# A list scheduler learns that VectorE and GpSimd share a port, and layer 1 takes its heads in another order

## The chip, the cores and the metric

The kernel runs on one core of one Trainium2 chip. The metric is the device time of one execution in microseconds (us), as the median of three runs. The profile's names for the engines are used throughout: PE is TensorE (its matrix products), PEld its weight loads, DVE is VectorE, ACT is ScalarE, POOL is GpSimd, SP is the queue that issues nearly all of the DMA transfers.

## The reference: what is computed

A trunk of two layers on a sequence of 512 rows of 1024 numbers, in float32. Both layers have the form

```python
h = rmsnorm(x, norm_mix[layer])
x = x + mixer(h)                       # even_mixer in layer 0, odd_mixer in layer 1
x = x + squared_relu_mlp(rmsnorm(x, norm_mlp[layer]), w_up[layer], w_down[layer])
```

and a last `rmsnorm` ends it. The part that matters here is the mixer of layer 1:

```python
qc, kc, vc, c_q, c_kv, k_r = split(h @ w_in)                 # 512, 512, 512, 384, 256, 32 columns
o_c = stick_breaking_attention(qc, kc, vc)                   # 8 heads of 64
q_full = rmsnorm(c_q, q_norm) @ w_uq                         # 8 heads of 64 + 32
kv_full = rmsnorm(c_kv, kv_norm) @ w_ukv                     # 8 heads of 64 + 64
o_d = mla_attention(q_nope, rope(q_rope), k_nope, rope(k_r), v_d)
o = concatenate([o_c, o_d]) @ w_out
# stick-breaking weights of a row: a = sigmoid(z) * (product of sigmoid(-z) over all later keys before the row)
```

`c_q` and `c_kv` are the latent compressions. The mixer of layer 0 has eight heads with a forgetting bias and eight with a relative-position bias, each with a softmax over its row.

## The kernel before, in words

**Numbers in two parts.** Products run on float32r operands, and each operand is kept as a rounded high part and the low part that is left, so a product of two matrices is three products on PE (`mm3`, L426). To make the two parts, ACT copies the high one and DVE subtracts it. For every 128x1024 block of weights that arrives by DMA as `wr`, this is one ACT copy to `wh` and one DVE subtraction to `wl` (`load_w`, L432). The blocks lie in a ring of eight buffers, so the split of a block waits until the products of an earlier one are done.

**The steps of layer 1.** The string `LAYER_1` (L29) is a list of names, and `step` (L1192) records the operations of each name:
- `v`: the values of the eight stick-breaking heads;
- `q0` to `q3` (`qk_pair`, L637): queries and keys of a pair of heads, 2 times 24 products of 512 columns;
- `s0` to `s7` (`stick_head`, L1171): one stick-breaking head. For each of four row blocks of 128 rows: two score products (`sc`) on PE, two sigmoids on ACT (`k` and `p`), two masks on POOL (AFFINE_SELECT), a running product along the row on DVE (a scan over `k`), and the product of `p` and `k` on POOL. Then ten transposes (`tr`) on PE, their split into two parts (`pt`) on ACT and DVE, eight products with the values (`av`), and the addition of the halves (`o`) on DVE;
- `cq` and `ck` (`c_proj`, L1110): the two compressions, 96 products of 384 columns and 96 of 288;
- `nq` and `nk` (`c_norm`, L1119): their norms, four row blocks each: a power of -1/2 of one number a row on POOL (`sm<-sm,mhalf`), a scaling on DVE (`ex<-u,sm,gain`), transposes on PE, a split (`u<-tr,u`);
- `kr`, `qr`, `qn`, `kn`, `vd`: rotated key, queries, keys and values of the latent heads from the normed compressions, with the weights of `wq` and `wkv`;
- `m0` to `m7`: the latent heads; `oc`, `od` and a last part ("end" below): the output projection; `x`: the residual is read back.

**What sets the order.** Nothing is issued as it is recorded. `Plan.schedule` (L133) is a list scheduler: it takes the recorded operations with their dependences, gives each engine the ready operation that was recorded first (those of the heads and norms count as 4000 places earlier, `urgent`), adds a cost from a table (`Op.cost`, L303), and frees buffers when their last use ends. The result is one fixed order for each engine, which then runs in that order: an operation that waits holds up all that stand behind it on its engine. The scheduler's times play no part on the chip; only its order does.

Of the kernel before, what the change touches and what calls it, by code (L numbers as in the profile page):

```python
# [25 lines left out]
WARM = 60  # L26
WARM2 = 12
LAYER_0 = """v a0 f0 f1 a1 a2 f2 f3 a3 f4 f5 f6 b0 f7 b1 c0 c1 b2 c2 b3 c3 x of c4 c5 c6 oc c7"""
LAYER_1 = """v cq q0 s0 nq ck s1 q1 kr s2 s3 nk q2 q3 wq qr0 qr1 qn0 qn1 qn2 qn3 wkv kn0 kn1 kn2 kn3 s4 s5 s6 vd0  # L29
 s7 vd1 vd2 vd3 x m0 m1 m2 m3 m4 m5 oc m6 od m7"""  # L30
Q_LORA, KV_LORA = 384, 256
NEG = -1.0e30
BIG = 3.0e38
# [25 lines left out]
class Plan:  # L59
# [73 lines left out]
    def schedule(self):  # L133
        self.depend()
        ops = self.ops
        for t in self.tag_of.values():
            if t.first is not None:
                t.slot.queue.append(t)
        for s in self.slots.values():
            s.queue.sort(key=lambda t: t.first)  # L140
        free_at = dict.fromkeys(self.ENGINES, 0.0)
        soon = {e: [] for e in self.ENGINES}
        ready = {e: [] for e in self.ENGINES}
        for i, op in enumerate(ops):
            if not op.left:
                heapq.heappush(soon[op.engine], (0.0, op.prio, i))
        order, dma_free, table = [], 0.0, None
        waiting = {}

        def wake(slot, now):  # L150
            for i in waiting.pop(slot, ()):
                heapq.heappush(soon[ops[i].engine], (now, ops[i].prio, i))

        while len(order) < len(ops):
            best = None
            for e in self.ENGINES:
                if ready[e]:
                    at = free_at[e]
                elif soon[e]:
                    at = max(free_at[e], soon[e][0][0])  # L160
                else:
                    continue
                if best is None or at < best[0]:
                    best = (at, e)
            assert best is not None, "the recorded order does not fit the tile pools"
            now, e = best
            while soon[e] and soon[e][0][0] <= now:
                _, p, i = heapq.heappop(soon[e])
                heapq.heappush(ready[e], (p, i))
            _, i = heapq.heappop(ready[e])  # L170
            op = ops[i]
            blocked = None
            fresh = [t for t in op.tiles if not t.placed]
            for t in fresh:
                s = t.slot
                if s.free_slots(now) <= 0 or (s.in_order and s.queue[s.head] is not t):
                    blocked = s
            if blocked is not None:
                late = blocked.next_free(now)
                if late is not None and (not blocked.in_order or any(  # L180
                        blocked.queue[blocked.head] is t for t in fresh)):
                    heapq.heappush(soon[e], (late, op.prio, i))
                else:
                    waiting.setdefault(blocked, []).append(i)
                continue
            for t in fresh:
                t.placed = True
                t.slot.take(now)
            cost = op.cost()
            if e == "scalar":  # L190
                want = TABLE.get(op.kw.get("func", op.args[2] if op.method == "activation" else None))
                if want is not None and want != table:
                    cost += 1300.0
                    table = want
            end = now + cost
            free_at[e] = end
            done = end
            if op.method == "dma_start":
                start = max(dma_free, end + 650.0)
                dma_free = start + op.dma_time()  # L200
                done = dma_free + 900.0
            order.append(i)
            for j in op.next:
                o = ops[j]
                lat = self.SEM if op.method == "dma_start" else self.LATENCY[e][o.engine]
                o.ready = max(o.ready, done + lat)
                o.left -= 1
                if not o.left:
                    heapq.heappush(soon[o.engine], (max(o.ready, now), o.prio, j))
            for t in fresh:  # L210
                wake(t.slot, now)
            for t in op.tiles:
                t.left -= 1
                t.end = max(t.end, done)
                if not t.left:
                    t.slot.give(t.end + self.SEM)
                    wake(t.slot, now)
        self.length = max(free_at.values())
        return order
# [68 lines left out]
class Op:  # L288
# [10 lines left out]

    def dma_time(self):  # L300
        return int(np.prod(self.outs[0].shape)) * 4 / 360.0

    def cost(self):  # L303
        if self.method == "dma_start":
            return 1000.0 if self.engine == "gpsimd" else 450.0
        n = self.width()
        if self.engine == "tensor":
            if self.method == "transpose":
                return 109.0
            m = int(np.prod(self.outs[0].shape[1:]))  # L310
            if self.outs[0].tensor.name.startswith("warm"):
                return 107.0
            return max(m / 2.4 + 13.5, 107.0)
        psum = any(a.space == bass.MemoryType.PSUM for a in self.ins)
        if self.engine == "scalar":
            c = n / 1.2 + (155.0 if n < 1024 else 140.0)
            if self.method == "activation" and isinstance(self.kw.get("bias"), bass.AP):
                c += 93.0
            return c + (188.0 if "accum_out" in self.kw else 0.0)
        if self.engine == "vector":  # L320
            if self.method in ("tensor_copy", "tensor_scalar", "memset") and not psum:
                return n / 1.92 + 100.0
            return n / 0.96 + (150.0 if n < 1024 else 100.0) + (83.0 if "accum_out" in self.kw else 0.0)
        if self.method == "tensor_tensor":
            return 599.0 if n == 1 else 2.1 * n + 150.0
        if self.method == "affine_select":
            return 430.0
        return 0.84 * n + (290.0 if self.method == "tensor_scalar" else 100.0)
# [45 lines left out]
def trunk(ctx, tc, x, positions, norm_mix, norm_mlp, norm_final, w_in_ab, b_forget, rel_bias,  # L374
# [888 lines left out]
    o = {}  # L1263
    for name in LAYER_1.split():
        step(name)
# [49 lines left out]
```

## Time and profile before

| | us |
|---|---|
| median of three runs | 1212.97 (1209.8 to 1214.74) |
| the profiled execution, its own time | 1213.36 |
| its span, first to last instruction | 1211.7 |
| PE busy | 1178.5 (97%) |
| DVE busy | 870.7 (72%) |
| ACT busy | 594.6 (49%) |
| POOL busy | 169.4 (14%) |

A busy PE is one that has a product under way; products are pipelined, so a PE that is busy can still be slower than it could be. In the trace nearly every operation has the line of the recording helper, so the names of what is written and read (`out<-in`) tell the operations apart. A stretch of the span can be asked for its busy times; layer 1's mixer lies between about 605 and 870 us.

### The profile page before, as it was taken

What the parts mean: (1) busy time and instruction counts of PE and PEld (TensorE: products, weight loads), DVE (VectorE), ACT (ScalarE), POOL (GpSimd) and SP (SyncE); (2) the same over time, 40 slices, a digit from 0 to 9 for tenths busy, and PEclk for the clock granted to TensorE, in tenths of its full rate; (3) what the DMA queues carried; (4) which work ended last, traced back from release to release, by engine and by line L of the source; (5) the groups of instructions that cost most, each with busy time, mean ns of one, the idle gap of its engine ahead of it and who ended that gap; (6) DMA issues with size and microseconds to landing.
All of it is one profiled execution on the core that took longest, in us unless ns stands there. A gap on an engine that the chain in (4) does not pass through costs nothing.

```text
span 1211.7 us, 16381 instructions
## 1 busy us (share of the span) xinstructions
PE 1178.5 (97%) x5958; PEld 993.0 (82%) x5958; DVE 870.7 (72%) x1466; ACT 594.6 (49%) x1064; POOL 169.4 (14%) x301
## 2 busy tenths in 40 slices
PE   9999999999999999999999998899899999999997
PEld 8987788888888888887899876688788888888886
DVE  6547788795876877777633899678768778787644
ACT  5346677534443444444424776556444434444423
POOL 2215522200000000000001576022100000000000
PEclk8999999999999999999999999899899999999999
DMA  5533334443143241225323212773521423321231
GB/s 196 158 96 96 88 93 162 137 151 121 35 139 105 74 153 43 62 70 160 111 76 100 79 53 72 171 197 77 207 86 39 156 85 98 128 69 36 72 102 70
DMA packets 101312, 127.89 MB, mean 106 GB/s; under 512 B 5272, under 2 KB 71200, under 8 KB 101232
## 3 DMA queue, kind: packets, MB, share of 16 engines
q1 hardware_dynamic: 101056, 126.55, 34.8%
q8 instruction: 47, 0.77, 0.3%
q0 software_dynamic: 176, 0.30, 0.1%
q14 instruction: 33, 0.27, 0.1%
HBM read 113.16 MB, written 4.23 MB: 97 GB/s over the span
## 4 chain that ended last, share of the span: by engine, by line
PE 64%; DVE 5%; DMA 3%; POOL 2%; issue 1%; ACT 1%; POOLq 0%; SPq 0%; DVEq 0%; ACTq 0%
PE mm L226 42%; PE pa L226 10%; PE pb L226 8%; POOL p L226 2%; PE tr L226 1%; DVE k L226 1%; PE sc L226 1%; PE av L226 1%; DVE wl L226 1%; DVE u L226 1%; DMA Qm<-u 1%; DVE pt L226 1%; DVE ex L226 1%; DMA Km<-u 1%; ACT wh L226 1%
## 5 line engine op out<-in xcount | busy, mean ns | idle before, releaser
L226 PE MATMUL mm<-u,wh 128*128 128x512 f32 (+1 forms) x1524 | 466.9, 384 | 4.1 <-DVE u L226 2.3
L226 PEld LDWEIGHTS mm<-u,wh 128*128 128x128 f32 x1524 | 279.7, 188 | 57.0 <-DVE u L226 4.4
L226 PE MATMUL mm<-u,wl 128*128 128x512 f32 (+1 forms) x762 | 292.2, 384 | 0.2 <-DVE wl L226 0.2
L226 PE MATMUL mm<-wh,u 128*128 128x512 f32 (+4 forms) x1008 | 269.6, 350 | 2.0 <-ACT u L226 2.0
L226 DVE TENSOR_TENSOR wl<-wr,wh 128x1024 fp32r<-128x1024 f32 (+5 forms) x152 | 175.3, 1157 | 88.2 <-ACT wh L226 86.5
L226 ACT CAST wh<-wr 128x1024 fp32r<-128x1024 f32 (+5 forms) x152 | 149.2, 987 | 156.2 <-PE mm L226 69.7
L226 PEld LDWEIGHTS mm<-wh,u 128*128 128x128 f32 x1008 | 178.3, 192 | 21.7 <-ACT u L226 2.3
L226 PE MATMUL mm<-wl,u 128*128 128x512 f32 (+4 forms) x504 | 177.0, 351 | 0.6 <-DVE wl L226 0.6
L226 PEld LDWEIGHTS mm<-u,wl 128*128 128x128 f32 x762 | 143.4, 188 | 26.2 <-DVE wl L226 0.9
L226 ACT CAST wh<-rw 128x1024 fp32r<-128x1024 f32 x84 | 88.5, 1054 | 114.3 <-PE mm L226 54.0
L226 DVE TENSOR_TENSOR wl<-rw,wh 128x1024 fp32r<-128x1024 f32 x84 | 102.8, 1223 | 57.0 <-ACT wh L226 56.5
L226 PEld LDWEIGHTS mm<-wl,u 128*128 128x128 f32 x504 | 96.9, 192 | 10.7 <-DVE wl L226 1.1
L226 POOL TENSOR_TENSOR sm<-sm,mhalf 128x1 f32<-128x1 f32 x28 | 21.4, 764 | 461.7 <-DVE sm L226 461.6
L226 POOL TENSOR_SCALAR p<-p,sm 128x128 f32<-128x128 f32 (+1 forms) x96 | 59.1, 616 | 177.1 <-DVE sm L226 143.8
L226 DVE TENSOR_TENSOR X<-mm,X 128x512 f32<-128x512 f32 x80 | 54.5, 686 | 30.4 <-PE mm L226 30.1
L226 PE MATMUL tr<-ident,p 128*128 128x128 f32 x320 | 65.3, 280 | 11.1 <-POOL p L226 10.7
L226 PE MATMUL pa<-wl,sh 128*128 128x512 f32 x192 | 74.7, 389 | 0.0
L226 PE MATMUL pa<-wh,sl 128*128 128x512 f32 x192 | 74.7, 389 | 0.0
L226 PE MATMUL pa<-wh,sh 128*128 128x512 f32 x192 | 74.4, 389 | 0.0
L226 ACT ACTIVATE sq<-ex 128x512 f32<-128x512 f32 x48 | 30.3, 630 | 86.3 <-DVE ex L226 86.3
L226 DVE SCALAR_TENSOR_TENSOR ex<-mm,rstd 128x512 f32<-128x512 f32 x64 | 44.0, 688 | 37.6 <-PE mm L226 33.7
L226 PE MATMUL av<-pt,u 128*128 128x512 f32 (+3 forms) x256 | 66.4, 342 | 0.6 <-ACT pt L226 0.5
(125 smaller groups left out, 1673.7 us busy)
## 6 DMA issues: line engine op xcount, KB each, us to landing
wr<-in_w_up_dram SPq DMA_DIRECT2D x64, 512.0 KB, 4.0
rw<-in_w_down_dram SPq DMA_DIRECT2D x48, 512.0 KB, 3.4
wr<-in_w_in_ab_dram SPq DMA_DIRECT2D x22, 512.0 KB, 4.2
wr<-in_w_down_dram SPq DMA_DIRECT2D x16, 512.0 KB, 3.3
wr<-in_w_in_cd_dram SPq DMA_DIRECT2D x11, 512.0 KB, 3.9
X<-in_x_dram SPq DMA_DIRECT2D x8, 512.0 KB, 6.2
wr<-in_w_out_ab_dram SPq DMA_DIRECT2D x8, 512.0 KB, 4.3
wr<-in_w_out_cd_dram SPq DMA_DIRECT2D x8, 512.0 KB, 4.2
```

The source lines that it names most:

```text
L226: getattr(getattr(self.nc, op.engine), op.method)(*op.args, **op.kw)
```

## The change

Two things, in one diff. The scheduler keeps a time `port_free`: an operation for which `Op.port` holds ends no earlier than `port_free - 200` ns plus its own cost, and then sets `port_free`. `port` holds for a GpSimd operation that reads a tile wider than one element a row from SBUF, and for a VectorE operation that reads two such tiles (one is enough for a copy or a scalar operation); tiles in PSUM don't count. And in `LAYER_1` the first two pairs of heads stand ahead of the compressions.

```diff
-LAYER_1 = """v cq q0 s0 nq ck s1 q1 kr s2 s3 nk q2 q3 wq qr0 qr1 qn0 qn1 qn2 qn3 wkv kn0 kn1 kn2 kn3 s4 s5 s6 vd0
- s7 vd1 vd2 vd3 x m0 m1 m2 m3 m4 m5 oc m6 od m7"""
+LAYER_1 = """v q0 s0 q1 s1 cq s2 nq ck s3 kr nk q2 s4 q3 wq qr0 qr1 qn0 qn1 qn2 qn3 wkv kn0 kn1 kn2 kn3 s5
+ vd0 vd1 vd2 vd3 s6 s7 x m0 m1 m2 m3 m4 m5 oc m6 od m7"""
...
-        order, dma_free, table = [], 0.0, None
+        order, dma_free, port_free, table = [], 0.0, 0.0, None
...
-            end = now + cost
+            if op.port():
+                end = max(now, port_free - 200.0) + cost
+                port_free = end
+            else:
+                end = now + cost
...
+    def port(self):
+
+        if self.engine not in ("vector", "gpsimd") or self.method == "dma_start":
+            return False
+        wide = [a for a in self.ins if a.space not in (bass.MemoryType.PSUM, bass.MemoryType.DRAM) and int(np.prod(a.shape[1:])) > 1]
+        return len(wide) > (self.engine == "vector" and self.method not in ("tensor_copy", "tensor_scalar"))
```

No operation is added or removed: both programs have the same 8871 recorded operations. On PE both start with the 192 products of `v`. Before, the row is `v`, the 96 of `cq`, the 48 of `q0`, then `ck`, among whose products the scores of `s0` and `s1` stand, then `q1`, `q2` with `s1` to `s3`, and `q3`, whose 14th product the scores of `s4` precede. Now it is `v`, `q0`, then `q1` and `cq` with `s0` to `s2` and the scores of `s3`, then `ck` with the rest of `s3`, then `q2`, and `q3`, of which 20 products stand ahead of the scores of `s4`. From `kn3` on both orders are nearly alike.

Three places. The first is POOL in layer 1. Before, the powers of `nq` (four rows of `sm<-sm,mhalf`) stand behind the last product of head `s1` (511 columns) and ahead of the masks of `s2`:

```order
L226 TENSOR_TENSOR p_1413<-p_1413,k_1414 128x383
L226 AFFINE_SELECT p_1416<-p_1416 128x128
L226 TENSOR_TENSOR p_1416<-p_1416,k_1417 128x511
L226 TENSOR_TENSOR sm_1370<-sm_1369,mhalf 128x1
L226 TENSOR_TENSOR sm_1376<-sm_1375,mhalf 128x1
L226 TENSOR_TENSOR sm_1382<-sm_1381,mhalf 128x1
L226 TENSOR_TENSOR sm_1388<-sm_1387,mhalf 128x1
L226 AFFINE_SELECT k_1444<-k_1444 128x128
L226 AFFINE_SELECT p_1443<-p_1443 128x128
```

Now they stand behind the last product of head `s3`, and the four of `nk` come right after them:

```order
L230 AFFINE_SELECT p_1463<-p_1463 128x128
L230 AFFINE_SELECT k_1467<-k_1467 128x128
L230 TENSOR_TENSOR p_1463<-p_1463,k_1464 128x383
L230 AFFINE_SELECT p_1466<-p_1466 128x128
L230 TENSOR_TENSOR p_1466<-p_1466,k_1467 128x511
L230 TENSOR_TENSOR sm_1420<-sm_1419,mhalf 128x1
L230 TENSOR_TENSOR sm_1426<-sm_1425,mhalf 128x1
L230 TENSOR_TENSOR sm_1432<-sm_1431,mhalf 128x1
L230 TENSOR_TENSOR sm_1438<-sm_1437,mhalf 128x1
L230 TENSOR_TENSOR sm_1487<-sm_1486,mhalf 128x1
```

What moved: the four powers wait for four heads where they waited for two.

The second place is DVE at the same point of the new order. The first row is the last scan of `s3` (a scan is printed as SCALAR_TENSOR_TENSOR on `k`), `ex<-u,sm,gain` is the scaling of `nq` that reads a power, and `wl` of 864 columns are the weights of `ck`:

```order
L230 SCALAR_TENSOR_TENSOR k_1467<-k_1467 128x512
L230 TENSOR_TENSOR o_1393<-av_1412,o_1393 64x512
L230 TENSOR_SCALAR sm_1419<-sm_1418 128x1
L230 SCALAR_TENSOR_TENSOR ex_1421<-u_1387,sm_1420,gain_1413 128x384
L230 TENSOR_TENSOR wl_1443<-wr_1441,wh_1442 128x864
L230 TENSOR_SCALAR sm_1425<-sm_1424 128x1
L230 TENSOR_TENSOR wl_1446<-wr_1444,wh_1445 128x864
L230 TENSOR_TENSOR u_1414<-tr_1422,u_1414 128x128
L230 TENSOR_TENSOR u_1415<-tr_1422,u_1415 128x128
```

Before, those weights stand between those of `q0` (the first two rows) and the halves of its queries and keys, ahead of all heads:

```order
L226 TENSOR_TENSOR wl_1337<-wr_1335,wh_1336 128x1024
L226 TENSOR_TENSOR wl_1341<-wr_1339,wh_1340 128x1024
L226 TENSOR_TENSOR wl_1393<-wr_1391,wh_1392 128x864
L226 TENSOR_TENSOR wl_1396<-wr_1394,wh_1395 128x864
L226 SCALAR_TENSOR_TENSOR Q_1227_1333<-mm_1338,Q_1227_1333 64x512 x2
L226 TENSOR_TENSOR wl_1399<-wr_1397,wh_1398 128x576
L226 TENSOR_TENSOR wl_1430<-wr_1428,wh_1429 128x1024
L226 TENSOR_TENSOR KL_1257<-mm_1342,KH_1334 64x512 x2
```

What moved: the weights of `ck` now stand behind the first scaling of `nq`, and so behind its power and `s3`.

The third place is DVE where head `s4` begins. Before, its four scans (`k_1570` to `k_1579`) stand among the last scalings and splits of `nk` and the weights of `wq` (`wl` of 512 and 128 columns):

```order
L226 SCALAR_TENSOR_TENSOR k_1570<-k_1570 128x128
L226 SCALAR_TENSOR_TENSOR ex_1506<-u_1401,sm_1505,gain_1481 128x256
L226 SCALAR_TENSOR_TENSOR k_1573<-k_1573 128x256
L226 TENSOR_TENSOR u_1482<-tr_1501,u_1482 128x128
L226 TENSOR_TENSOR u_1483<-tr_1501,u_1483 128x128
L226 TENSOR_TENSOR wl_1533<-wr_1531,wh_1532 128x512
L226 TENSOR_TENSOR u_1482<-tr_1507,u_1482 128x128
L226 TENSOR_TENSOR u_1483<-tr_1507,u_1483 128x128
L226 SCALAR_TENSOR_TENSOR k_1576<-k_1576 128x384
L226 SCALAR_TENSOR_TENSOR k_1579<-k_1579 128x512
L226 TENSOR_TENSOR wl_1533<-wr_1531,wh_1532 128x128
```

Now these stand ahead of its first scan (`k_1521`), all but three of the weights' splits:

```order
L230 TENSOR_TENSOR wl_1546<-wr_1544,wh_1545 128x1024
L230 TENSOR_TENSOR wl_1550<-wr_1548,wh_1549 128x512
L230 TENSOR_TENSOR KL_1256<-mm_1517,KH_1509 64x512 x2
L230 TENSOR_TENSOR wl_1550<-wr_1548,wh_1549 128x128 x2
L230 TENSOR_TENSOR wl_1553<-wr_1551,wh_1552 128x512
L230 TENSOR_TENSOR wl_1553<-wr_1551,wh_1552 128x128 x2
L230 SCALAR_TENSOR_TENSOR k_1521<-k_1521 128x128
L230 SCALAR_TENSOR_TENSOR k_1524<-k_1524 128x256
L230 SCALAR_TENSOR_TENSOR Q_1432_1538<-mm_1543,Q_1432_1538 64x512
L230 SCALAR_TENSOR_TENSOR k_1527<-k_1527 128x384
L230 SCALAR_TENSOR_TENSOR k_1530<-k_1530 128x512
```

What moved: between the first scan of `s4` and the first split of `kn` DVE has eight operations fewer, five of `nk` and three of `wq`.

## Rows read from the trace of the kernel before

**Rows 1.** The profile's page, its first part: busy us of an engine, share of the span, number of instructions.
```profile
PE 1178.5 (97%) x5958; PEld 993.0 (82%) x5958; DVE 870.7 (72%) x1466; ACT 594.6 (49%) x1064; POOL 169.4 (14%) x301
```

**Rows 2.** Busy time by stretches of 25 us, four of them: the stretch and its length, busy us of PE, PEld, DVE, ACT and POOL (with the number of instructions), the granted clock of PE as a share of full speed, the share of the DMA engines, GB/s.
```profile
125.00:150.00 25.00, 23.34 (x123) 19.14 (x124) 17.46 (x49) 16.27 (x36) 15.14 (x30) 1.00 0.41 106
...
700.00:725.00 25.00, 22.66 (x118) 17.56 (x116) 24.06 (x46) 19.00 (x54) 18.84 (x29) 1.00 0.23 64
725.00:750.00 25.00, 22.16 (x114) 16.56 (x114) 24.09 (x37) 17.88 (x42) 18.69 (x37) 1.00 0.18 53
...
900.00:925.00 25.00, 25.00 (x112) 20.68 (x112) 19.58 (x23) 11.24 (x14) 0.00 (x0) 1.00 0.07 21
```

**Rows 3.** Who waited for whom, PE, 700 to 765 us: us in total, times, the longest.
```profile
PE tr L226 <- POOL p L226: 5.5, 6, 1.6
```

**Rows 4.** The same, PE, 75 to 160 us (layer 0).
```profile
PE tr L226 <- POOL p L226: 3.2, 5, 0.8
```

**Rows 5.** The same, PE, 765 to 785 us.
```profile
PE sc L226 <- DMA Km<-u: 3.0, 1, 3.0
```

**Rows 6.** Busy time by stretches of 5 us, columns as in rows 2.
```profile
770.00:775.00 5.00, 3.29 (x11) 3.00 (x12) 2.35 (x6) 3.31 (x5) 0.06 (x1) 0.64 0.79 179
...
845.00:850.00 5.00, 3.16 (x17) 2.06 (x15) 2.81 (x7) 2.15 (x7) 1.28 (x2) 0.99 0.47 133
850.00:855.00 5.00, 3.33 (x10) 2.51 (x10) 2.41 (x4) 1.68 (x4) 0.00 (x0) 0.67 1.05 392
```

**Rows 7.** Busy time of three stages, columns as in rows 2: heads `s0` and `s1`, heads `s2` and `s3`, and from the first scan of `s4` to the first split of `kn`.
```profile
661.30:679.40 18.10, 18.10 (x121) 16.97 (x120) 13.46 (x21) 13.08 (x31) 15.44 (x25) 1.00 0.22 58
...
692.60:710.90 18.30, 16.44 (x86) 12.50 (x84) 17.77 (x24) 12.92 (x33) 14.89 (x24) 1.00 0.09 24
...
718.60:765.40 46.80, 40.12 (x199) 29.71 (x197) 43.79 (x70) 30.50 (x71) 27.13 (x47) 1.00 0.35 88
```

**Rows 8.** The trace of PE in order of time: start us, us, the operation, how many follow each other, and in brackets the idle time before. These are the first products of `cq`, `q0` and `ck`, the first score of `s0`, the first product of `q1`, three transposes of `nq` and what follows them, the first score of `s4`, and the last block of transposes of `m7`.
```profile
629.53 0.34 PE L226 MATMUL mm<-wh,u 128*128 128x384 f32 x1
...
646.17 0.63 PE L226 MATMUL mm<-u,wh 128*128 128x512 f32 x2
...
657.09 0.29 PE L226 MATMUL mm<-wh,u 128*128 128x288 f32 x1
...
661.33 0.23 PE L226 MATMUL sc<-KH,Q 128*128 128x128 f32 x1
...
674.59 0.63 PE L226 MATMUL mm<-u,wh 128*128 128x512 f32 x2
...
689.55 0.49 PE L226 MATMUL tr<-ident,ex 128*128 128x128 f32 x3
689.87 0.60 PE L226 MATMUL tr<-ident,p 128*128 128x128 f32 x4
...
714.93 0.22 PE L226 MATMUL sc<-KH,Q 128*128 128x128 f32 x1
...
848.98 0.55 PE L226 MATMUL tr<-ident,p 128*128 128x128 f32 x3 [1.36 <-POOL p L226]
```

**Rows 9.** The same of POOL: the first mask of `s0`, a later mask of it, the last product of `s1`, the first power of `nq`, the first mask of `s2`, the last product of `s3`, the first mask of `s4`, the last two products of `s7`.
```profile
662.54 0.29 POOL L226 TENSOR_SCALAR_AFFINE_SELECT k<-k 128x128 f32<-128x128 f32 x1 [53.37 <-ACT k L226]
...
667.98 1.21 POOL L226 TENSOR_SCALAR_AFFINE_SELECT k<-k 128x128 f32<-128x128 f32 x1
...
677.30 2.10 POOL L226 TENSOR_TENSOR p<-p,k 128x511 f32<-128x511 f32 x1
679.36 0.54 POOL L226 TENSOR_TENSOR sm<-sm,mhalf 128x1 f32<-128x1 f32 x1
...
693.41 0.29 POOL L226 TENSOR_SCALAR_AFFINE_SELECT k<-k 128x128 f32<-128x128 f32 x1 [5.42 <-ACT k L226]
...
709.76 1.09 POOL L226 TENSOR_TENSOR p<-p,k 128x511 f32<-128x511 f32 x1 [1.22 <-DVE k L226]
...
715.71 0.29 POOL L226 TENSOR_SCALAR_AFFINE_SELECT k<-k 128x128 f32<-128x128 f32 x1 [1.12 <-ACT k L226]
...
748.92 3.12 POOL L226 TENSOR_TENSOR p<-p,k 128x383 f32<-128x383 f32 x2 [1.16 <-DVE k L226]
```

**Rows 10.** The same of DVE: the first two scans of `s0`, its last scan with what follows, the first scan of `s2`, the first scan of `s4`, the first three splits of `kn`.
```profile
662.86 1.31 DVE L226 TENSOR_TENSOR_SCAN k<-k 128x128 f32<-128x128 f32 x2 [1.70 <-POOL k L226]
...
667.79 1.86 DVE L226 TENSOR_TENSOR_SCAN k<-k 128x512 f32<-128x512 f32 x2
...
694.04 0.42 DVE L226 TENSOR_TENSOR_SCAN k<-k 128x128 f32<-128x128 f32 x1
...
718.66 0.42 DVE L226 TENSOR_TENSOR_SCAN k<-k 128x128 f32<-128x128 f32 x1
...
764.67 1.89 DVE L226 TENSOR_TENSOR u<-mm,u 128x512 fp32r<-128x512 f32 x3 [1.04 <-ACT u L226]
```

**Rows 11.** Groups of DVE's operations between 711 and 740 us: operation, count | busy us, mean ns of one | idle before. The first two are splits of `wq`'s weights, the third the scaling and the fourth the splits of `nk`.
```profile
L226 DVE TENSOR_TENSOR wl<-wr,wh 128x128 fp32r<-128x128 f32 x6 | 3.0, 512 | 0.0
...
L226 DVE TENSOR_TENSOR wl<-wr,wh 128x512 fp32r<-128x512 f32 x3 | 2.1, 708 | 0.0
...
L226 DVE SCALAR_TENSOR_TENSOR ex<-u,sm,gain 128x256 f32<-128x256 f32 x4 | 1.9, 478 | 0.1
L226 DVE TENSOR_TENSOR u<-tr,u 128x128 fp32r<-128x128 f32 x8 | 1.9, 279 | 0.0
```

## The prediction

> **What bounds the kernel now.** I read the first part of the page first: PE has a product under way for 1178.5 of 1211.7 us [rows 1]. So at most 33 us of the span can come from better order, and the question is where PE is idle. The stretches of 25 us answer that: in the MLPs PE is full (25.00 of 25 at 900) and no order can gain there, while in 700 to 750 it is idle for 2.3 and 2.8 us a stretch, with DVE at 24.1 of 25 [rows 2]. In layer 0, at 125 to 150, it is idle for 1.7 us. Next the waits: in 700 to 765 PE's transposes of the stick-breaking weights wait six times for POOL's products, 5.5 us in all [rows 3]; in layer 0 five times, 3.2 us [rows 4]; and the first scores of the latent heads wait 3.0 us for a transfer to `Km` [rows 5]. Behind that wait, and again at 850, the granted clock of a stretch of 5 us is 0.64 and 0.67 [rows 6]: a part of the stretch ran at 1.2 instead of 2.4 GHz.
>
> Who holds POOL up is seen in its own rows: a mask takes 0.29 us where DVE does no scan, and 1.21 us where one runs beside it [rows 9, 10]. The two engines do delay each other, as the change assumes. While heads `s4` to `s7` run, DVE is busy 43.8 of 46.8 us and POOL 27.1, and PE is idle for 6.7 [rows 7]. So in that stage the end is set by DVE and POOL together; in the stage of `s0` and `s1` PE is full and hides the heads.
>
> **The change, step by step.** The sum is made against the profiled execution, 1213.36 us; the median of the runs is 1212.97, so 0.4 lower. No operation is added or removed; only order changes.
>
> *1. The heads begin earlier.* Before, `cq` (16.64 us, 629.53 to 646.17) stands ahead of `q0` (10.92, to 657.09), and the first score follows 4.24 later, at 661.33 [rows 8]. Now `cq` stands behind: 661.33 - 16.64 = 644.7 for the first score, and the first mask 1.2 later, as now [rows 8, 9], at 645.9.
>
> *2. How long four heads take.* From the first mask to the last product, `s0` and `s1` take 662.54 to 679.40 = 16.9 us, `s2` and `s3` 693.41 to 710.85 = 17.4 [rows 9]. In the first of these DVE is busy for 13.5 of 18.1 us [rows 7], so there is room for the splits of `cq`'s weights beside them; as some of those share the port I add 1 us (an estimate from the 0.71 us of a 512-wide split [rows 11] and one or two that fall badly). Then `s3` ends at 645.9 + 34.3 + 1 = 681.2. The powers of `nq` now stand behind that. One takes 0.54 [rows 9], the scaling of the row about 0.5 [rows 11], and with 0.5 for the handovers the first transposes of `nq` can begin at 682.7.
>
> *3. When PE would be there.* Prices from PE's rows: 48 products of 512 columns in 10.92 us are 0.2275 each, 96 of 384 columns in 16.64 are 0.173, 32 of `ck` in 4.24 are 0.1325 [rows 8]. Between 657.09 and 674.59 stand 96 products of `ck` (12.7) and 34 products and transposes of heads, for which 4.7 is left: 0.138 each. Ahead of `nq`'s transposes PE now has `q0` and `q1` (21.8), 88 products of `cq` (15.25), and 86 products of heads (26 for each of `s0` to `s2`, 8 scores of `s3`; 11.9). Without a wait it would be there at 629.5 + 49.0 = 678.5. So PE waits 4.2 us, behind which `ck`'s products stand, too. Bounds: none, if the heads run 4 us faster; 8, if they run as much slower.
>
> *4. From there to `s4`.* A transpose of `nq` takes a third of 689.55 to 689.87, 0.107 [rows 8]. 12 of `nq` and 8 of `nk` are 2.1, the last 8 of `cq` 1.4, `ck` 12.7, 18 products of `s3` 2.5, `kr` 0.4 (three or four products), `q2` 10.9, 20 products of `q3` 4.55: together 34.6. So the first score of `s4` falls at 682.7 + 34.6 = 717.3, where it is at 714.93 [rows 8]: +2.4. Without the wait of step 3 it would be at 713.1.
>
> *5. From `s4` to `kn`.* Now 50.4 us lie between that score and the end of the first split of `kn`, 764.67 + a third of 1.89 = 765.3 [rows 8, 10]. Seen from DVE, which is nearly full there: its first scan comes 3.7 us after the score (718.66), at `s0` 1.5 after (662.86 against 661.33) [rows 8, 10]; with the operations of `nk` out of the way I expect the latter: -2.2. Eight operations fewer stand in between, one scaling at 0.48, four splits at 0.28, one split of 512 columns at 0.71 and two of 128 at 0.51 [rows 11]: -3.3. Together -5.5. Seen from POOL, `s4` to `s7` take 715.71 to 752.04 = 36.3 us, where the first four take 34.3 [rows 9]: -2.0. Which of the two ends last cannot be read, and I take a value near the middle, -3.9. `kn` then comes 1.5 earlier than before.
>
> *6. Behind `kn`* the order is the same, so I cost the wait for `Km` and the clock behind it [rows 5, 6] at nothing. It is covered by no work: if `kn` comes early and the transfer doesn't follow, all of step 5 is lost.
>
> *7. Layer 0.* The new rule also reorders the forgetting heads. At stake are the 3.2 us [rows 4]. The most is -3.2; a worse order could cost about one such wait more, +1. I take -1.2, nearer to nothing than to all, since the pieces of work stay as long as they are and only their order among each other changes.
>
> *8. The end of layer 1.* `m7`'s last transposes wait 1.36 us for POOL [rows 8], in a stretch where PE is busy 3.16 of 5 and the clock falls right behind it [rows 6]. Now 14 products stand between the last score of `m7` and its last transposes, where 8 stood. Six at 0.2275 are 1.37, which covers the wait: -1.4. If the idle time behind it goes too (5 - 3.33 = 1.67 us in 850 to 855 [rows 6]) it is -3.0; if the moved products themselves come late, +0.5 (a third of the present wait).
>
> Sum: +2.4 - 3.9 - 1.2 - 1.4 = -4.1 us, 1209.3 for a profiled execution and 1208.9 for the median; I say **1209**.
>
> **The rivals.** *The port itself binds.* The mask at 1.21 us [rows 9] is not faster for standing elsewhere; the work of both engines on the port is the same in any order. Then step 5 is worth POOL's -2.0 only and layer 0 nothing: +2.4 - 2.0 - 1.4 = -1.0, about **1212**. For it: two heads take nearly the same time in two stages (16.9 and 17.4 us [rows 9]), though DVE is full in one and three quarters busy in the other [rows 7]. Against it: POOL itself is idle for 20 of 46.8 us while `s4` to `s7` run. The Trainium skill, page "SBUF — State Buffer", section "Who interferes with whom", has a rule that speaks for this rival: a DVE instruction with two inputs in SBUF and a GpSimd instruction that reads SBUF exclude each other, and the second one blocks fully until the first ends. The trace agrees as to the mask. By the rule alone, the order decides who is blocked but not how much is done in all, and the time would be that of this rival.
>
> *The heads are slower where they have no cover, and the compressions stand behind them (slower).* Over all eight, a head takes (752.04 - 661.33)/8 = 11.3 us [rows 8, 9]. At this pace `s3` ends at 645.9 + 45.4 = 691.3, `nq` begins at 692.8, and `s4` at 727.4, 12.5 late; with POOL's -2.0 and the -1.4 of the end the sum is +9, about **1222**. For it: `nq`, `ck` and `nk` now all hang on POOL's last product of `s3`, and the splits of `ck`'s weights stand on DVE behind the first scaling. Against it: the 11.3 hold two gaps in which POOL had nothing to do (5.42 us ahead of `s2` [rows 9]). It ends slower than before when `s4`'s first score falls later than 714.9 + 3.9 + 2.6 = 721.4, and by over 0.5% from 727.5 on.
>
> *All of it works.* No wait at `nq` (713.1, so -1.8), DVE's -5.5, layer 0's -3.2 and the end's -3.0 give -13.5, about **1200**; half of the surplus over the forecast is likelier than all of it, which is about 1204.
>
> **How the numbers follow.** Runs of this kernel lie within 5 us of each other, so 0.5%, 6.1 us, is about what a measurement can tell: below 1206.9 is faster, above 1219.0 slower. The forecast (1205 to 1212) has a chance of 0.45, the port that binds 0.20, the slow heads 0.15, all of it working 0.20. Faster: all of it working, and a third of the forecast's case, 0.35. Slower: the slow heads and a little more, 0.16. The rest, 0.49, can't be told from no change. The range leaves out the slow heads and the last few us of the best case: 1199 to 1218.
>
> **What would show it.** Step 1: the first score of `s0` near 645. Steps 2 and 3: POOL's last product of `s3` near 681, and an idle time of PE of about 4 us ahead of `nq`'s first transposes, released by DVE's `ex`; if it is 10 or more, the slow heads are right, and with none the best case. Step 4: `s4`'s first score at about 717. Step 5: the first split of `kn` ending near 764; if POOL's `s4` to `s7` still take 36 us and PE still waits 5 us for POOL's `p`, the port binds. Step 6: the wait for `Km` still near 3.0 us. Step 7: less than 3.2 us of waits for `p` between 75 and 160. Step 8: no wait at `m7`'s last transposes. What would make the forecast wrong most easily is step 2, as everything up to `s4` hangs on the pace of four heads in a place where they have never stood.

## The result and the profile after

The changed kernel takes **1199.23 us** (median of six runs, 1197.72 to 1201.2), beside 1212.1 us for the kernel before on the same chip (1209.8 to 1214.74); the ratio is 0.9893, 95% interval 0.9877 to 0.991. So it is faster by 1.1%, inside the range of 1199 to 1218 but at its lower edge, and 10 us better than the 1209 that I took. The profiled execution has a span of 1199.5 us.

The profile's page, its first part, as in [rows 1]:

```profile
PE 1170.9 (98%) x5958; PEld 992.3 (83%) x5958; DVE 872.1 (73%) x1466; ACT 593.6 (49%) x1064; POOL 166.0 (14%) x301
```

PE's trace, with the operations of [rows 8]: the first score of `s0`, the first transposes of `nq`, the first score of `s4`, and further the first score of `m0` and the last transposes of `m7`.

```profile
641.26 0.22 PE L230 MATMUL sc<-KH,Q 128*128 128x128 f32 x1
...
675.97 0.49 PE L230 MATMUL tr<-ident,ex 128*128 128x128 f32 x3
...
711.57 0.30 PE L230 MATMUL sc<-KH,Q 128*128 128x128 f32 x1 [0.47 <-ACT wh L230]
...
763.63 0.33 PE L230 MATMUL sc<-Km,Qm 96*128 96x128 f32 x1 [1.63 <-DMA Km<-u]
...
836.41 0.55 PE L230 MATMUL tr<-ident,p 128*128 128x128 f32 x3 [0.97 <-POOL p L230]
```

POOL's, as in [rows 9] (first mask of `s0`, last product of `s1`, last product of `s3` with the first power of `nq`, first mask of `s4`, last two products of `s7`), and DVE's first two scans of `s4` and first splits of `kn`, as in [rows 10]:

```profile
641.98 0.29 POOL L230 TENSOR_SCALAR_AFFINE_SELECT k<-k 128x128 f32<-128x128 f32 x1 [37.49 <-ACT k L230]
...
658.30 1.09 POOL L230 TENSOR_TENSOR p<-p,k 128x511 f32<-128x511 f32 x1
...
673.39 1.09 POOL L230 TENSOR_TENSOR p<-p,k 128x511 f32<-128x511 f32 x1
674.45 0.55 POOL L230 TENSOR_TENSOR sm<-sm,mhalf 128x1 f32<-128x1 f32 x1
...
712.37 0.39 POOL L230 TENSOR_SCALAR_AFFINE_SELECT k<-k 128x128 f32<-128x128 f32 x1 [16.03 <-ACT k L230]
...
741.87 3.12 POOL L230 TENSOR_TENSOR p<-p,k 128x383 f32<-128x383 f32 x2 [1.30 <-DVE k L230]
```
```profile
712.79 1.30 DVE L230 TENSOR_TENSOR_SCAN k<-k 128x128 f32<-128x128 f32 x2 [0.19 <-POOL k L230]
...
758.01 1.89 DVE L230 TENSOR_TENSOR u<-mm,u 128x512 fp32r<-128x512 f32 x3 [0.93 <-ACT u L230]
```

PE's waits, in layer 0 (75 to 160 us, as in [rows 4]), and from 697 to 757 us (as in [rows 3]):

```profile
PE tr L230 <- POOL p L230: 1.4, 2, 0.7
```
```profile
PE tr L230 <- POOL p L230: 3.2, 3, 1.7
```

The waits for POOL's products have fallen from 3.2 to 1.4 and from 5.5 to 3.2 us; 1.63 us remain of the wait for `Km`, which was 3.0 [rows 5]. Stretches of 5 us, as in [rows 6], around 745, behind `Km` and at the end of the mixer:

```profile
745.00:750.00 5.00, 4.45 (x16) 3.49 (x17) 3.54 (x7) 1.50 (x4) 0.00 (x0) 0.66 0.64 105
...
765.00:770.00 5.00, 5.00 (x25) 4.17 (x24) 3.50 (x13) 3.69 (x9) 0.85 (x2) 1.00 0.42 139
...
840.00:845.00 5.00, 2.96 (x7) 2.39 (x8) 1.81 (x3) 1.19 (x2) 0.00 (x0) 0.62 1.04 388
845.00:850.00 5.00, 5.00 (x19) 3.99 (x19) 3.42 (x7) 1.94 (x5) 0.01 (x1) 0.70 1.05 386
```

Behind `Km` the clock is full (1.00 where 0.64 stood); at 745 it is now low where it was not.

**Where the time went.** Each trace is cut at six places: first product of layer 0's heads, first product of layer 1's values `v`, first score of `s4`, end of the first split of `kn`, end of the last product of `vd3`, first transpose ahead of the last MLP. Each kernel was profiled twice (the second executions are E11 and E12 below); a cell holds both, in us.

| stretch | predicted | before | after | difference of the means |
|---|---|---|---|---|
| layer 0 and its MLP | -1.2 | 539.8, 539.0 | 536.1, 536.4 | -3.1 |
| `v` to `s4` | +2.4 | 110.2, 111.6 | 110.1, 110.3 | -0.7 |
| `s4` to `kn` | -3.9 | 50.4, 50.4 | 47.1, 48.3 | -2.7 |
| `kn` to `vd3` | 0 | 16.1, 13.4 | 11.1, 9.8 | -4.3 |
| `vd3` to the last MLP | -1.4 | 79.3, 78.5 | 78.8, 76.2 | -1.5 |
| last MLP and norm | 0 | 347.1, 347.1 | 347.1, 347.1 | 0 |

The largest gain lies where I had put nothing.

### The profile page after: what moved, and what is told of

Same layout as the page of the kernel before. It is cut to its first block, busy times and chain, and to the rows that moved or that the text cites. A ratio compares the mean times of both kernels' runs of the same rounds, so it can differ in the third digit from the quotient of the medians.

```text
span 1199.5 us, 16367 instructions
## 1 busy us (share of the span) xinstructions
PE 1170.9 (98%) x5958; PEld 992.3 (83%) x5958; DVE 872.1 (73%) x1466; ACT 593.6 (49%) x1064; POOL 166.0 (14%) x301
## 4 chain that ended last, share of the span: by engine, by line
PE 71%; DVE 3%; DMA 1%; ACT 1%; issue 1%; POOL 0%; POOLq 0%; DVEq 0%; ACTq 0%
PE mm L230 46%; PE pa L230 11%; PE pb L230 8%; PE sc L230 2%; PE tr L230 2%; PE av L230 1%; DVE u L230 1%; DVE ex L230 1%; DVE wl L230 1%; DVE k L230 1%; DMA wr<-in_w_down_dram 0%; DMA Km<-u 0%; DVE pt L230 0%; DMA wr<-in_w_uq_dram 0%; ACT wh L230 0%
## 5 line engine op out<-in xcount | busy, mean ns | idle before, releaser
L230 PE MATMUL mm<-wh,u 128*128 128x512 f32 (+4 forms) x1008 | 272.4, 352 | 2.0 <-ACT u L230 2.0
L230 DVE TENSOR_TENSOR wl<-wr,wh 128x1024 fp32r<-128x1024 f32 (+5 forms) x152 | 173.9, 1150 | 76.8 <-ACT wh L230 76.4
L230 POOL TENSOR_SCALAR p<-p,sm 128x128 f32<-128x128 f32 (+1 forms) x96 | 53.5, 558 | 174.4 <-DVE sm L230 146.6
L230 DVE TENSOR_TENSOR pt<-tr,pt 128x512 fp32r<-128x512 f32 (+1 forms) x96 | 54.6, 596 | 16.5 <-ACT pt L230 15.6
```

What stands on the lines that cost most here:

```text
L230: getattr(getattr(self.nc, op.engine), op.method)(*op.args, **op.kw)
```

## The experiments

Each run is set beside runs of the kernel before on its own chip (median 1211.32 us for E1 to E4, 1213.15 for E5 to E8, 1211.78 for E9 and E10), so that across chips the ratios count and not the medians. "Layer 0" and "mixer 1" are the first row of the table above and the four next ones together (for before 539.8 and 256.0, second execution 539.0 and 254.0; for the change 536.1 and 247.1, second 536.4 and 244.6).

| run | list | scheduler | layer 0 | mixer 1 | median | ratio, 95% interval |
|---|---|---|---|---|---|---|
| E1 | old | port rule | 537.3 | 257.6 | 1211.63 | 0.9996 (0.9979 to 1.0013) |
| E2 | new | as before | 539.1 | 252.0 | 1208.23 | 0.9982 (0.9966 to 0.9999) |
| change | new | port rule | 536.1 | 247.1 | 1199.23 | 0.9893 (0.9877 to 0.991) |
| E3 | new | wrong rule | 534.4 | 251.4 | 1203.73 | 0.9933 (0.9911 to 0.9955) |
| E5 | new | POOL dearer | 533.5 | 245.9 | 1197.2 | 0.987 (0.9851 to 0.989) |
| E8 | new | wrong rule in layer 0, port rule behind | 533.8 | 245.8 | 1196.81 | 0.9864 (0.9849 to 0.988) |
| E9 | old | POOL dearer | 534.6 | 248.0 | 1198.0 | 0.9889 (0.9867 to 0.9911) |
| E10 | new | POOL dearer and port rule | 542.8 | 261.1 | 1221.27 | 1.009 (1.0064 to 1.0117) |

**E1: the rule alone.** The changed scheduler with the old `LAYER_1`.

> The scheduler's port rule with the old list of steps. Theory (each part works in a place of its own): layer 0 is that of the change, so the first products of layer 1's values come 3.3 us earlier than before (601.5 instead of 604.8); in layer 1 the order of the steps is the old one, so the wait for Km and the half clock behind it (8.2 us from the end of kn's first split to the first score of m0 and its slow products) stay. About 1209, between 1207 and 1210. Rival (the two parts only work together, since the rule helps where heads stand close): layer 0's 3.3 us and a loss in layer 1 of as much, 1212. Rival (the rule does nearly all): below 1203.

The rival's number holds: layer 0 gains 2 us, mixer 1 loses as much, and the ratio is 0.9996. (Its reason fails: E5 and E9 below get the gain without the rule.) `s4`'s first score comes 3.9 us earlier after `v` than before (106.3), but from there to `kn` it takes 55.5 us instead of 50.4, so `kn` ends 161.8 us after `v`, where it was 160.6 and 162.0: heads that started earlier here ended no earlier. The loss itself lies from `vd3` to the last MLP (81.1 for 79.3 and 78.5), where the clock is low from 847 to 858 in this trace.

**E2: the list alone.** The old scheduler with the new `LAYER_1`.

> The new list of steps with the old scheduler. Theory: layer 0 as before (values of layer 1 at 604.8), heads s0 to s3 covered by cq and q1 as with the change, first score of s4 within 1 us of 714.9, the 3.3 us from s4 to kn and the 5 us behind kn gained: about 1204, between 1202 and 1206. Rival (without the rule the masks stand beside scans and the heads take 11 us each): s4's first score later than 719 and 1210 or more.

`s4`'s place is as the theory said (715.3), and `s4` to `kn` takes 47.0 us, 3.5 less than before. But the 5 us behind `kn` are not there: `kn` to `vd3` takes 15.1. So 3 us of the 12.9 are the list's by the medians (2.2 by the ratio), none are the rule's, and the sum is far from the change's. What is more in the change lies mostly in layer 0 (3 us) and behind `kn`. There the queue shows it. These are the issues on SP of the first two weight blocks of the output projection and of `m0`'s keys behind them, in E2, before, and after:

```profile
759.75 1.62 SPq L226 DMA_DIRECT2D wr<-in_w_out_cd_dram  x2
762.26 1.14 SPq L226 DMA_DIRECT2D Km<-u  x2
```
```profile
762.45 1.59 SPq L226 DMA_DIRECT2D wr<-in_w_out_cd_dram  x2
765.39 1.14 SPq L226 DMA_DIRECT2D Km<-u  x2
```
```profile
754.58 2.91 SPq L230 DMA_DIRECT2D wr<-in_w_out_cd_dram  x2
758.73 0.49 SPq L230 DMA_DIRECT2D Km<-u  x1
```

The weights are issued 2.5, 2.9 and 4.2 us ahead of the keys, and PE's wait for `Km` is 2.5, 3.0 and 1.6 us. The lead alone does not set the wait: second executions with the same leads (E11 and E12, below) wait 1.3 us less. In step with the wait goes the time from issue to landing, in us, of the second weight block (512 KB) and of the keys behind it (256 KB); in E4, the next run, the keys stand ahead of the weights.

| | before | E11 | E2 | change | E12 | E4 |
|---|---|---|---|---|---|---|
| second weight block | 7.0 | 5.5 | 6.1 | 5.6 | 3.3 | behind |
| keys | 6.3 | 5.0 | 5.9 | 4.9 | 3.6 | 3.2 |
| PE's wait for `Km` | 3.0 | 1.7 | 2.5 | 1.6 | 0.3 | 0.15 |

Why the same block takes 7.0 us in one execution and 5.5 in another is not seen.

**E4: is it the weights?** The kernel before, with those two blocks held back (`mark` copies one column of `kn3`'s split into the buffer).

```diff
+        if late is not None:
+            mark(raw, late)
         nc.sync.dma_start(dst, view)
...
-            add_proj(X, oC, 4, w_out_cd, 0)
+            add_proj(X, oC, 4, w_out_cd, 0, late=f32(KN[3][:, 1, 0:1]))
```

> The kernel before, with the first two weight blocks of the output projection (512 KB each) held back until kn3 is split, so that m0's Km transfers stand ahead of them on the queue (two tiny copies on DVE are added). Theory (the wait for Km is the transfers' share of the DMA engines, and the half clock is that wait's): the wait of 3.0 us falls below 1.5, the clock stays at full speed between 771 and 778, the end comes 4 to 6 us earlier, about 1208, unless the projection waits for its weights. Rival (the chain from kn3's split over a transfer to m0 takes 3 us by itself): wait and half clock stay, 1212 to 1214.

The mechanism of the wait holds, the time does not: 1214.13 us (ratio 1.0019, 1.0006 to 1.0033). PE's first score of `m0` waits 0.15 us, and no low clock follows (`kn` to `vd3` 10.2 us). But the third block is late now, ACT waits for it, and PE for the transposed softmax weights (`pt`), which stand behind that split on ACT:

```profile
769.80 0.41 PE L226 MATMUL sc<-Km,Qm 96*128 96x128 f32 x2 [0.15 <-issue]
```
```profile
783.40 1.04 ACT L226 CAST wh<-wr 128x1024 fp32r<-128x1024 f32 x1 [3.44 <-DMA wr<-in_w_out_cd_dram]
```
```profile
784.99 0.50 PE L226 MATMUL av<-pt,u 128*128 128x512 f32 x1 [2.41 <-ACT pt L226]
```

`vd3` to the last MLP takes 85.3 us instead of 79.3. The wait was moved, not removed, and behind the moved one the clock is low (785 to 790). Behind `kn` the order on PE, ACT and DVE shifts too, so E4 does more than hold the weights back.

**E3: a wrong rule.** Does the rule help because it is true? Here the scheduler believes that ACT and POOL share a port.

```diff
-        if self.engine not in ("vector", "gpsimd") or self.method == "dma_start":
+        if self.engine not in ("scalar", "gpsimd") or self.method == "dma_start":
...
-        return len(wide) > (self.engine == "vector" and ...)
+        return len(wide) > 0
```

> The change with a wrong rule: the scheduler believes that ACT and POOL share a port, which nothing in the trace shows. Theory (the rule helps because DVE and POOL do delay each other): layer 0 gains nothing (values of layer 1 at 604 to 606), in all 1203 to 1208 like the new list alone. Rival (any rule that spreads POOL's work out gives another order, and the gain in layer 0 is that of another order): values of layer 1 near 601.5 and 1199 to 1201.

In layer 0 the rival holds and more: 5 us are gained, where the right rule gains 3. The rows say how. Before, POOL's scaling of the second row block and DVE's split of a weight block start together, and PE's next transpose waits:

```profile
123.59 1.52 POOL L226 TENSOR_SCALAR p<-p,sm 128x256 f32<-128x256 f32 x1
```
```profile
123.58 1.26 DVE L226 TENSOR_TENSOR wl<-wr,wh 128x1024 fp32r<-128x1024 f32 x1
```
```profile
125.16 0.33 PE L226 MATMUL tr<-ident,p 128*128 128x128 f32 x1 [0.44 <-POOL p L226]
```

It was so at 103.05 and 113.31, and comes back at 133.63 and 143.97. The groups of that scaling from 75 to 165 us, for before, after, and E5:

```profile
L226 POOL TENSOR_SCALAR p<-p,sm 128x256 f32<-128x256 f32 x8 | 9.1, 1134 | 1.0 <-DVE sm L226 1.0
```
```profile
L230 POOL TENSOR_SCALAR p<-p,sm 128x256 f32<-128x256 f32 x9 | 6.3, 699 | 5.2 <-DVE sm L230 5.2
```
```profile
L226 POOL TENSOR_SCALAR p<-p,sm 128x256 f32<-128x256 f32 x8 | 3.8, 475 | 8.1 <-DVE sm L226 8.0
```

The right rule takes most of these collisions out (1134 ns falls to 699). But POOL then meets the splits with other operations, as here with a mask, which takes 0.29 us alone:

```profile
132.67 1.27 POOL L230 TENSOR_SCALAR_AFFINE_SELECT p<-p 128x128 f32<-128x128 f32 x1
```
```profile
132.52 1.27 DVE L230 TENSOR_TENSOR wl<-wr,wh 128x1024 fp32r<-128x1024 f32 x1
```

Counted from 75 to 165 us:

| | before | change | E3 | E5 |
|---|---|---|---|---|
| POOL operations of over 1.2 us beside a split of weights | 5 | 4 | 4 | 2 |
| of these, the scaling of 256 columns | 5 | 2 | 1 | 0 |
| PE's waits for `p` | 5 | 2 | 0 | 0 |

So the order changes less how often the two engines meet than which operation is held up, and PE's waits follow the scaling alone. Under the wrong rule a collision with it is left in head `f5`, but eight products of PE instead of three stand between that head's first two transposes, and PE does not wait for the second:

```profile
130.97 1.44 POOL L230 TENSOR_SCALAR p<-p,sm 128x256 f32<-128x256 f32 x1
```
```profile
132.64 0.27 PE L230 MATMUL tr<-ident,p 128*128 128x128 f32 x1
```

**E5: only later.** No rule at all; POOL's masks, products and scalings cost 400 ns more in the table.

```diff
-            return 599.0 if n == 1 else 2.1 * n + 150.0
+            return 599.0 if n == 1 else 2.1 * n + 550.0
...
-            return 430.0
-        return 0.84 * n + (290.0 if self.method == "tensor_scalar" else 100.0)
+            return 830.0
+        return 0.84 * n + (690.0 if self.method == "tensor_scalar" else 100.0)
```

> The new list of steps, no rule about a port; instead each of POOL's masks, products and scalings costs 400 ns more in the scheduler's table. Theory (the scheduler of before believed POOL's results to be there sooner than they are, and whatever makes them later in its plan puts more products on PE ahead of the transposes that wait): the values of layer 1 start at 599 to 602 instead of 604, in all 1200 to 1205. Rival (it takes a rule about two engines at once): the values start at 603.5 to 605 and the time is that of the new list alone, 1207 to 1209.

Better than the theory: 1197.2 us. PE waits for no `p` from 75 to 160 us, and the scaling meets no split any more, though no rule forbids it (475 ns, above). In mixer 1 it goes another way than the change: the first split of `kn` ends at 748.7, 12 us ahead of `s7`'s last product on POOL, which ends at 761.0; with the change `s7` ends at 745.0 and `kn` comes behind it at 758.7.

```profile
748.05 0.69 DVE L226 TENSOR_TENSOR u<-mm,u 128x512 fp32r<-128x512 f32 x1
```
```profile
759.95 1.08 POOL L226 TENSOR_TENSOR p<-p,k 128x511 f32<-128x511 f32 x1
```

So the latent heads begin ahead of the end of the last stick-breaking head (first score of `m0` at 754.7), where with the change they begin behind it (763.6).

**E8: the wrong rule in layer 0, the right one behind it.**

> The change with the wrong rule (ACT and POOL share a port) for the operations recorded ahead of layer 1's first step, and the right one behind. Theory (the gains of the places add): the values of layer 1 start near 599.4, 2 us earlier than with the change, the rest is the change's: 1197, between 1195.5 and 1198.5. Rival (what is gained in layer 0 is lost behind, as a wait for Km of over 2 us with half clock or at m7): 1199 to 1202.

The theory holds in this run: the gains of the places add. 1196.81 us is the lowest median of all; its interval touches that of the change, so that it beats the change is likely and not shown beyond doubt.

**E9: the old list with the dearer table.**

> The old list of steps with POOL's dearer table and no rule about a port. Theory (what is late in the scheduler's plan decides, and the list matters little once POOL's lateness is known to it): layer 0 as with the dearer table (values of layer 1 near 598.4), and a good part of the gain in layer 1 too: 1198 to 1203. Rival (the list carries the gain in layer 1, as the port rule alone gained nothing there): layer 0's 6 us and no more, 1205 to 1209.

The theory holds, 1198.0 us. With POOL's lateness in the table the old list is as good as the new one (E5), and here too `kn`'s split (750.0) precedes `s7`'s last product (766.3). Neither part of the change is needed for the gain.

**E10: both corrections.**

> The change (new list, right rule) with POOL's dearer table as well. Theory (rule and dearer table say the same thing twice, that POOL is late): layer 0 as with the dearer table alone or a little worse, in all 1196 to 1199. Rival (they add): 1194 or less. Rival (too much lateness puts the heads' products too far behind, and layer 1's mixer waits for its heads): 1201 or more.

The second rival holds, 1221.27 us: too much of it. At the end of layer 0 PE now waits (200 to 265 us; before and with the change no wait there is over 0.7), and in mixer 1 the heads are late (61.3 us from `s4` to `kn`).

```profile
PE tr L230 <- POOL p L230: 3.1, 1, 3.1
PE mm L230 <- ACT u L230: 2.0, 1, 2.0
```

**E7: more cover for the heads.** The change with `q2` ahead of `s2` and `ck` behind `s4` in the list (`v q0 s0 q1 s1 q2 s2 cq s3 nq s4 ck kr nk q3 s5 wq ...`).

> The change with q2 ahead of s2 too, and ck behind s4, so that s4 begins while PE still has ck and q3. Theory (heads cost nothing where PE has other products, and PE's idle time of the change lies where s6 and s7 have none left): s4's first score by 700 instead of 711.6, PE idle for 4 us less between s4 and kn, 1195 to 1198. Rival (DVE is full from s4 to kn and sets the end in any order): kn's first split within 1.5 us of 758.7, 1198 to 1202. Rival (nk and wq come late and kn with them): 1203 or more.

Inconclusive. `s4` begins at 674.6 and `kn`'s split ends at 755.0, 3.7 us earlier than with the change, as the theory wanted; but four runs lie between 1199.33 and 1206.73 with a median of 1204.16 (ratio 0.992, 0.9889 to 0.995), and the profiled one is the fastest of them. Where the others lose is not seen.

**E6: the wait for `Km` made longer.** The change, with this transfer made twice; an operation in `unseen` costs nothing in the scheduler's plan:

```diff
+        if h == 0:
+            nc.unseen.add(len(nc.ops))
+            move(K[0:64], KN[pr][half])
         move(K[0:64], KN[pr][half])
```

> The change, with the transfer to m0's Km made twice, one behind the other, without the scheduler knowing, so that every engine's order stays. Theory (the half clock of the kernel before follows from the long wait for Km): the wait goes from 1.6 us to about 4.5, and the clock falls to half for some 7 us behind it, as before; vd3 ends 6 us later relative to kn's first split (17 instead of 11), about 1205. Rival (the clock falls for another reason): the wait alone, 14 us and about 1202. Rival (the wait isn't on the path): 1199 to 1200.

The median is the theory's, 1205.23 us (ratio 0.9932, 0.9916 to 0.9948), and the trace denies the theory. The wait is 2.60 us, longer than E2's 2.5, and no low clock follows it; stretches of 2.5 us:

```profile
765.00:767.50 2.50, 0.40 (x2) 0.00 (x0) 0.96 (x1) 1.47 (x2) 0.00 (x0) 1.00 0.68 133
767.50:770.00 2.50, 2.00 (x13) 1.90 (x14) 1.36 (x6) 1.06 (x3) 0.24 (x1) 1.00 0.94 251
770.00:772.50 2.50, 2.50 (x12) 2.06 (x12) 1.21 (x2) 1.16 (x5) 0.14 (x1) 1.00 0.65 246
```

`kn` to `vd3` takes 12.1 us, 1.6 more than the change's mean; the other 4 us lie in layer 0, in `s4` to `kn` and at the end, where the clock is low in this trace (271 to 276, 742 to 754 and 841 to 853 us). The mean clock of all four runs is low, too (0.987 to 0.990 of full speed, beside 0.991 to 0.996 in E5 and E8 on the same chip); why is not seen. E6 also does more than lengthen the wait: three products of the output projection now stand ahead of `m0`'s first scores, and the queue issues the second copy at 764.78, when the first, of 761.45, has landed. What the longer wait itself does to the median is not settled.

**E11 and E12: both kernels profiled again.**

> The kernel before, a second profiled execution. Theory (the wait for Km and the half clock behind it belong to this order): m0's first score about 6.3 us behind the end of kn's first split, clock at half between 771 and 778, vd3's end 16 us behind that split. Rival (the half clock falls differently in each execution): it stands elsewhere, and vd3's end is 12 to 14 us behind the split.

> The changed kernel, a second profiled execution. Theory: as in the first, the wait for Km is 1.6 us and no half clock follows it, vd3's end 11 us behind kn's first split. Rival (that the clock stayed up there was chance): half clock behind Km, 14 us.

Both times something of each. Before, the wait is 1.7 us here, and a shorter low stretch follows:

```profile
770.00:772.50 2.50, 1.33 (x7) 1.33 (x8) 0.74 (x3) 2.48 (x3) 0.00 (x0) 0.81 1.00 204
772.50:775.00 2.50, 2.50 (x8) 2.11 (x8) 1.70 (x5) 0.74 (x3) 0.38 (x1) 0.50 0.72 196
775.00:777.50 2.50, 2.50 (x12) 1.99 (x11) 1.32 (x5) 1.67 (x4) 0.48 (x1) 1.00 0.41 159
```

After, it is 0.3 us, and the clock stays full:

```profile
PE sc L230 <- DMA Km<-u: 0.3, 1, 0.3
```

So each order keeps its kind (low clock behind `Km` in both executions of before, in neither of after), while the wait itself moves by 1.3 us from one execution to the next. In E12 the clock is low ahead of `kn` instead, from 740 to 751 us, where the first execution had it low from 745 to 750.

## Why the prediction was right in sign and too small

**Steps 1 to 4, the heads' new place.** Step 1 holds: 641.26 is 3.4 us ahead of the 644.7 worked out, and 3.2 of these come from ahead of layer 1, whose first product stands at 601.51 instead of 604.75. Step 2 was too slow: from the first mask to the last product four heads take 641.98 to 674.48 = 32.5 us, not 35.3. With that the wait of 4.2 us in step 3 falls away: `nq`'s transposes stand at 675.97 with no idle time ahead, where PE without a wait was put at 678.5 less those 3.2, 675.3. (In step 3 itself 17.5 less 12.7 leaves 4.8 us for the 34 products, not 4.7; this is 0.2 us in the sum.) The step that failed is the pace of `s2` and `s3`. It was taken from a stage in which DVE was busy for 17.77 of 18.30 us [rows 7]; here it is busy for 14.34 of 16.30:

```profile
658.20:674.50 16.30, 16.30 (x104) 15.82 (x104) 14.34 (x20) 11.82 (x31) 15.05 (x27) 1.00 0.01 2
```

The two heads take 15.1 us (659.39 to 674.48) instead of 17.4. `s0` and `s1` take 17.4, for 16.9 and the added 1 us. From `nq` to `s4` it takes 35.6 us for the 34.6 of step 4. So +2.4 became -0.7. The slow rival is refuted by the same rows: `s3` ends at 674.5, not at 688.

**Step 5** is -2.7 for -3.9. The split between its two views was wrong: POOL's `s4` to `s7` fell from 36.3 to 712.37 to 744.99 = 32.6 us, more than the 2.0 that I allowed. Of DVE's 5.5 the first part came (the first scan follows the score by 1.2 us instead of 3.7), the second did not: from that scan to the end of the split it takes 45.9 us and in E12 47.1, for 46.7 before. In this stretch the clock is now low, which it was not before (next step).

**Step 6 is the term that was mis-sized**: nothing, where -4.3 was measured. I wrote that the order behind `kn` is the same, which it is, and forgot what else is on the queue: the weights' place ahead of the keys follows from when DVE frees their buffers, and that did move. The queue's own waits, before (760 to 773 us) and after (753 to 765):

```profile
SPq L226 <- DVE wl L226: 2.0, 3, 0.7
```
```profile
SPq L230 <- DVE wl L230: 3.0, 3, 2.1
```

E4 shows the cause of the wait. The wait accounts for 1.4 of the 4.3 us (means 2.4 and 1.0). Most of the rest is the clock, and the clock did not get better so much as fall elsewhere. What PE loses to it in each stretch, in us (an estimate: PE's busy time in each us, times the share of full speed that its row lacks; PE also waits there, so not all of it need be lost to the end):

| stretch | before | E11 | after | E12 |
|---|---|---|---|---|
| `s4` to `kn` | 0 | 0 | 1.6 | 3.9 |
| `kn` to `vd3` | 3.2 | 1.7 | 0 | 0 |
| `vd3` to the last MLP | 3.3 | 1.7 | 3.0 | 0 |

So a part of what `kn` to `vd3` won, step 5 paid. How much of the place of the low clock belongs to the order rests on two executions each and on E2, and E6 speaks against a simple rule.

**Step 7** is -3.1 for -1.2, just inside its bound. The reason that I gave for taking little, that the pieces stay as long as they are, was wrong for the one piece that PE waits for: the scaling falls from 1134 to 699 ns on the mean. For POOL as a whole it was nearly right: from 65 to 600 us it is busy for 65.1 us before, 63.8 with the change and 63.3 in E5. So the port rival had the work on the port about right and its worth wrong. The Trainium skill's page "SBUF — State Buffer", section "Who interferes with whom", says that who comes second blocks until the first has ended. The trace nearly agrees (1.52 us where it takes 0.48 alone, so 1.04 more, beside a split of 1.26 that started 0.01 us earlier). I had concluded that order cannot help. But order decides which operation loses, and who waits for the loser.

**Step 8** has the size (-1.5 for -1.4) by chance. The six products do stand there, and the wait fell only from 1.36 to 0.97 us. The rest is the clock: less the last row of the table above the stretch takes 76.0 and 76.8 us before, 75.8 and 76.2 after.

**What the rule does** is in the end not what it says. E1, E3, E5 and E9 show that a true rule gains nothing with the old list, that a wrong rule gains more in layer 0, and that 400 ns on POOL's costs without any rule gain as much as the whole change, with either list. What all gains seem to share is that PE and DVE are given more to do ahead of what waits for POOL. That this is the cause is the simplest reading of these runs; for layer 0 the counts under E3 bear it out, for mixer 1 it is argued and not shown. E10 shows that it has an end.

## What to carry to other kernels

A fixed order made from a table of costs is only as good as the lateness that the table knows: look in the trace for the operation that takes three times its usual time in the same place of round after round, and tell the planner that its result comes late, before a model of the cause is built. Of a wait that a change does not touch, ask what stands ahead of it on its queue and when that gets its buffer. And try the two halves of a change and a false twin of its rule: here they showed that the rule need not be true, and E5 and E9 that neither half is needed for the gain.

## What the runs showed of the hardware

POOL's scaling of 128x256 takes 0.48 us alone and 1.52 beside a split on DVE that started 0.01 us earlier. A transfer of 256 KB landed 3.2 us after its issue with no weights ahead of it on the queue (E4), and 3.6 to 6.3 us behind two blocks of 512 KB. The 2.4 GHz clock of PE falls to 1.2 in stretches that differ between two executions of one kernel (before, 771 to 779 and 849 to 861 us in the first, 771 to 775 and 853 to 857 in the second), each costing 1.6 to 3.9 us by the estimate above, in two traces of each kernel; a wait of 1.7 us was followed by one (E11), and a wait of 2.6 by none (E6). What decides it is open.
